# Evictions into column order, walked rows outside before and columns outside after

## The chip, the cores and the metric

The kernel runs on one core of a Trainium2 chip. The metric is the device time in microseconds (us). Three runs of the kernel before gave 1960.73, 1961.32 and 1965.41 us; their median is 1961.32 us.

## The reference

One encoder layer on 1024 tokens of width 1024, in fp32. One input projection gives queries, keys and values for two attention branches and two gates. Branch A is a 2-D neighbourhood attention: the 1024 tokens are a grid of 16 rows and 64 columns, and each query sees a window of 8 rows by 16 columns. Branch B is a windowed attention over token order. The gated sum goes through an output projection and a layer norm, and then a mixture of 16 experts with a second layer norm.

```
proj = einsum('bsd,de->bse', x, w_in) + b_in
qa, ka, va, qb, kb, vb, ga, gb = split(proj)
ya = neighbourhood_attention(qa, ka, va, rpb)      # tokens as 16 rows x 64 columns
yb = windowed_gqa(qb, kb, vb, sink)
mix = sigmoid(ga) * (ya @ w_branch_a) + sigmoid(gb) * (yb @ w_branch_b)
h   = layer_norm(alpha * x + mix @ w_out)
out = layer_norm(alpha * h + expert_choice_moe(h))
```

## The kernel before, in words

Every large product is made in three passes of float32r matmuls: an operand is split into a high part, rounded to float32r, and a low part, the rest; high x high, high x low and low x high are added in one PSUM bank. So each operand has to be written twice: ScalarE (ACT) writes the high part, and VectorE (DVE) then subtracts it from the source and writes the low part.

The first part of the kernel, up to about 575 us, makes the projections and both attentions at once. A unit of projection (`proj`, L183) is 24 matmuls of 512 columns into one PSUM tile `pj` of a pool of two (`pp`), so the next unit but one cannot start before the evictions of a unit have been read. `fill(n)` puts n projection matmuls between two steps of the attentions; the order on TensorE (PE) is that of the program, while ACT and DVE are ordered by the framework's scheduler. Branch B's steps come first, those of branch A after them, and the projections for branch A's four head pairs (i = 0 to 3) run beside the attention steps before they are needed.

Branch A wants its tokens in column order: position 16 * column + row, so that 128 neighbouring positions are 8 whole columns of the grid. The projection gives row order. The reordering is done by the evictions: `pj` for half `nh` holds rows 8 * nh to 8 * nh + 7, each of 64 columns, so that one column's eight rows lie 64 floats apart in PSUM and next to each other in the SBUF tile. The evictions concerned are

- `kside` (L208 ACT writing `khh`, L210 DVE writing `kll`): for each key unit and each of its halves of 64 partitions two ACT and two DVE instructions of 512 elements; a tile with keys of branch B (`kB`) uses the same lines without a reordering;
- `qside` (L217 ACT, L218 DVE, writing `qs`): for each query unit four of each with 256 elements; the queries of branch B have 512 elements in plain order;
- `va_unit` (L281 ACT, writing `vta`): one instruction of 512 elements in all 128 partitions for each value unit.

After the attentions, `y_load` (L595 ACT writing `yh`, L596 DVE writing `yl`) brings branch A's result back to row order while it is split, from SBUF to SBUF, in four tiles of 128 x 1024. Branch B's four tiles go through the same lines in plain order.

Of the kernel before, what the change touches and what calls it, by code (L numbers as in the profile page):

```python
# [21 lines left out]
HD = 64  # L22
GRID = 64
# [31 lines left out]
def encoder_block(ctx, tc, x, w_in, b_in, rpb, sink, w_branch_a, w_branch_b, w_out, ln1_g, ln1_b,  # L55
# [21 lines left out]
    def f32(ap):  # L77
        return ap.bitcast(F32)
# [98 lines left out]
    def proj(c, nh):  # L177
        hi, lo = held["w", c]
        ps = pp.tile([P, 512], F32, name="pj")
        n = 0  # L180
        for a, part in ((hi, "hi"), (hi, "lo"), (lo, "hi")):
            for k in range(KD):
                nc.tensor.matmul(ps, a[:, k, :], xT[part, nh][:, k, :], start=(n == 0), stop=(n == 3 * KD - 1))  # L183
                n += 1
                yield ps
# [10 lines left out]


    def by_column(ap, nh):
        return ap.rearrange("p (c r) -> p r c", r=16)[:, 8 * nh:8 * nh + 8, :]

    def by_row(ap):
        return ap.rearrange("p (r c) -> p r c", c=GRID)

    def kside(ps, c, half, khh, kll, view, src_view):
        lo, hi = half * HD, (half + 1) * HD
# [7 lines left out]
    def qside(src, c, half, qs, view):  # L213
        lo, hi = half * HD, (half + 1) * HD
        o = 1 - half
        b = bcol[lo:hi, c:c + 1]
        nc.scalar.activation(view(qs[lo:hi]), src, AF.Identity, bias=b)  # L217
        nc.vector.scalar_tensor_tensor(view(qs[o * HD:(o + 1) * HD]), src, b, f32(view(qs[lo:hi])),  # L218
                                       op0=ALU.add, op1=ALU.subtract)

    def k_unit(key, c, nh):
        if nh == 0:
            held[key] = ([qkv.tile([P, S], F32R, name="khh", tag="k", bufs=6) for _ in range(2)],
                         [qkv.tile([P, S], F32R, name="kll", tag="k", bufs=6) for _ in range(2)])
        for ps in proj(c, nh):
            yield
        for half in range(2):
            if key == "kB":
                v, sv = lambda ap: ap[:, nh * 512:(nh + 1) * 512], lambda ap: ap
            else:  # L230
                v, sv = lambda ap: by_column(ap, nh), by_row
            kside(ps, c, half, held[key][0][half], held[key][1][half], v, sv)
        done.add((key, nh))
# [11 lines left out]
    def qa_unit(key, c, nh):  # L245
        if nh == 0:
            held[key] = {(half, g): qkv.tile([P, 512], F32R, name="qs", tag="q", bufs=8)
                         for half in range(2) for g in range(2)}
        for ps in proj(c, nh):
            yield  # L250
        for half in range(2):
            for g in range(2):
                src = by_row(ps[half * HD:(half + 1) * HD])[:, :, 32 * g:32 * g + 32]
                qside(src, c, half, held[key][half, g], lambda ap: by_column(ap, nh))
        done.add((key, nh))

# [18 lines left out]
    def va_unit(key, c, nh):  # L275
        if nh == 0:
            held["vt", key] = vtp.tile([P, S], F32, name="vta")
        vt = held["vt", key]
        for ps in proj(c, nh):
            yield  # L280
        nc.scalar.activation(by_column(vt, nh), by_row(ps), AF.Identity, bias=bcol[:, c:c + 1])  # L281
        if nh:
            later.append([8, lambda: v_split(key, vt, 0, [(key, 0)])])
            later.append([14, lambda: v_split(key, vt, 4, [(key, 1)])])
# [37 lines left out]
    def qkv_units(i):  # L322
        return units(qa_unit, ("q", i), i) + units(k_unit, ("k", i), 4 + i) + units(va_unit, ("v", i), 8 + i)
# [184 lines left out]
    for r in range(16):  # L508
# [3 lines left out]
                                    ap=[[15 * 31, 8], [1, 8 * 31]]))  # L512
# [75 lines left out]
    def y_load(nm, src):  # L588
        for k in range(4):
            raw = gp.tile([P, S], F32, name="yraw", tag="g")  # L590
            nc.sync.dma_start(raw, src[k * P:(k + 1) * P, :])
            s0, hi, lo = raw, yT[nm][0][k], yT[nm][1][k]
            if nm == "a":
                s0, hi, lo = raw.rearrange("p (c r) -> p r c", r=16), by_row(hi), by_row(lo)
            nc.scalar.activation(hi, s0, AF.Copy)  # L595
            nc.vector.tensor_tensor(lo, s0, f32(hi), op=ALU.subtract)  # L596

    y_load("b", yb_d)
    wbr = {}

# [43 lines left out]

    gate("b", 0)
    y_load("a", ya_d)
    for d in range(0, 8, 2):
        work = [(nm, d + u) for u in range(2) for nm in ("b", "a")]
# [586 lines left out]
    def stats(t):  # L1235
        z, stt = total(t), stat.tile([P, 16], F32, name="ln")
        for h in range(2):
            nc.vector.bn_stats(stt[:, 6 * h:6 * h + 6], z[h])  # L1238
        yield
        nc.vector.bn_aggr(stt[:, 12:14], stt[:, :12].rearrange("p (c k) -> p c k", k=6))  # L1240
        yield
        nc.vector.tensor_scalar(stt[:, 14:15], stt[:, 13:14], EPS, None, op0=ALU.add)
        nc.gpsimd.tensor_tensor(stt[:, 15:16], stt[:, 14:15], mhalf, op=ALU.pow)
        yield
        for h, sl in enumerate(halves):
            nc.vector.scalar_tensor_tensor(accs[t][:, sl], z[h], stt[:, 12:13], g2[:, sl], op0=ALU.subtract,  # L1246
                                           op1=ALU.mult)
            if h == 0:
                yield
        yield  # L1250
        if t in TX:
            nc.scalar.activation(accs[t], accs[t], AF.Copy, scale=stt[:, 15:16])
            (nc.gpsimd if t in TP else nc.vector).tensor_tensor(accs[t], accs[t], b2, op=ALU.add)
        for sl in halves if t not in TX else [slice(0, D)]:
            if t not in TX:
                nc.vector.scalar_tensor_tensor(accs[t][:, sl], accs[t][:, sl], stt[:, 15:16], b2[:, sl], op0=ALU.mult,  # L1256
                                               op1=ALU.add)
            (nc.scalar if t % 2 else nc.sync).dma_start(out2[t * P:(t + 1) * P, sl], accs[t][:, sl])
        yield

    with tc.manual_schedule(engines=MAN):
        g = [stats(t) for t in range(8)]
# [30 lines left out]
```

## Time and profile before

| | |
|---|---|
| median of three runs | 1961.32 us |
| profiled execution | 1960.38 us, its span 1958.6 us |
| PE busy | 1863.8 us, 95% of the span |
| DVE, ACT, POOL busy | 1482.2, 1222.5, 221.3 us |
| projections and attentions | about 0 to 575 us |
| branches, mixing, first layer norm, routing | about 575 to 820 us |
| experts and the end | about 820 to 1958 us |

The table is read from the top: PE is busy nearly all the time, so what counts is where it waits or runs slowly. Those places are found in the stretches of the span and in the list of its waits.

### The profile page before, as it was taken

The page shows a single profiled execution, that of the slowest core. Times are in us where ns is not written, and L with a number is a line of the kernel's source. Part 1 is how long each engine was busy: PE and PEld are TensorE (multiplying, and loading weights), DVE is VectorE, ACT ScalarE, POOL GpSimd, SP SyncE. Part 2 cuts the span into 40 slices and gives each one's busy share as a digit, 9 for nine tenths or more (in the row PEclk, how much of TensorE's full clock was granted, in tenths as well). Part 3 has the DMA queues.
Part 4 walks back from the last instruction along what each step waited for, and adds up shares of the span by engine and source line. Part 5 has one row for each costly group of instructions (what it writes and reads, how often), then busy time and mean ns, then how long its engine had stood idle before and what let it go on. Part 6 is the DMA issues. An engine that isn't in the chain of part 4 may idle for free.

```text
span 1958.6 us, 23860 instructions
## 1 busy us (share of the span) xinstructions
PE 1863.8 (95%) x8795; PEld 1532.0 (78%) x8795; DVE 1482.2 (76%) x1857; ACT 1222.5 (62%) x1319; POOL 221.3 (11%) x271
## 2 busy tenths in 40 slices
PE   7998998988999999499999999999999999999996
PEld 6886877876877787388888888888888888888884
DVE  5466655554444558889989998998899899899897
ACT  4456655565444411277777777777777777777772
POOL 2121121111102222000000000000000000000003
PEclk9999999999999999699999999999999999999998
DMA  7111122222155274679999999999999999999982
GB/s 247 49 60 43 54 73 59 71 68 60 60 167 199 97 272 158 255 282 363 387 389 389 371 393 393 375 384 389 387 373 387 394 382 384 384 383 382 389 318 86
DMA packets 177129, 507.08 MB, mean 259 GB/s; under 512 B 12690, under 2 KB 55956, under 8 KB 177012
## 3 DMA queue, kind: packets, MB, share of 16 engines
q1 hardware_dynamic: 158816, 465.60, 63.5%
q0 software_dynamic: 7888, 24.13, 4.4%
q10 hardware_dynamic: 10308, 15.82, 2.4%
q8 instruction: 69, 1.13, 0.2%
q14 instruction: 48, 0.39, 0.1%
HBM read 468.40 MB, written 37.09 MB: 258 GB/s over the span
## 4 chain that ended last, share of the span: by engine, by line
PE 56%; DVE 2%; DMA 1%; issue 0%; ACT 0%; DVEq 0%; ACTq 0%
PE gu L1090 35%; PE yb L1090 18%; PE mt L1070 2%; PE gu L1098 1%; DMA xg<-h_d,idx 0%; DVE ln L1238 0%; DVE raw L1246 0%; DVE raw L1256 0%; DMA acc_d<-xr 0%; PE gu L1229 0%; PE mt L982 0%; DVE srt L752 0%; DVE srt L740 0%; DVE srt L750 0%; DVE srt L741 0%
## 5 line engine op out<-in xcount | busy, mean ns | idle before, releaser
L1053 DVE TENSOR_TENSOR mlo<-raw,mhi 128x2048 fp32r<-128x2048 f32 x383 | 859.1, 2277 | 52.8 <-PE yb L1090 26.0
L1045 ACT ACTIVATE mhi<-raw 128x2048 fp32r<-128x2048 f32 x383 | 732.3, 1912 | 200.3 <-PE gu L1090 93.7
L1090 PE MATMUL gu<-mhi,xsh 128*128 128x512 f32 x1008 | 398.2, 395 | 0.0
L1090 PE MATMUL gu<-mhi,xsl 128*128 128x512 f32 x1008 | 393.0, 390 | 0.0
L1090 PE MATMUL gu<-mlo,xsh 128*128 128x512 f32 x1008 | 393.0, 390 | 0.0
L1090 PEld LDWEIGHTS gu<-mhi,xsl 128*128 128x128 f32 x1008 | 189.5, 188 | 39.8 <-DVE xsl L1073 0.2
L1090 PEld LDWEIGHTS gu<-mlo,xsh 128*128 128x128 f32 x1008 | 189.7, 188 | 37.3
L1090 PEld LDWEIGHTS gu<-mhi,xsh 128*128 128x128 f32 x1008 | 189.6, 188 | 37.5 <-ACT xsh L1072 0.2
L1090 PE MATMUL yb<-mhi,hsl 128*128 128x512 f32 x512 | 199.4, 389 | 0.0
L1090 PE MATMUL yb<-mhi,hsh 128*128 128x512 f32 x512 | 199.3, 389 | 0.0
L1090 PE MATMUL yb<-mlo,hsh 128*128 128x512 f32 x512 | 199.2, 389 | 0.0
L183 PE MATMUL pj<-xThi,whi 128*128 128x512 f32 x544 | 157.1, 414 | 20.6 <-DVE kll L210 16.2
L183 PE MATMUL pj<-xTlo,whi 128*128 128x512 f32 x544 | 153.3, 405 | 0.0
L183 PE MATMUL pj<-xThi,wlo 128*128 128x512 f32 x544 | 151.3, 402 | 0.0
L183 PEld LDWEIGHTS pj<-xThi,whi 128*128 128x128 f32 x544 | 101.2, 195 | 43.9 <-issue 15.6
L183 PEld LDWEIGHTS pj<-xThi,wlo 128*128 128x128 f32 x544 | 99.3, 189 | 19.1
L183 PEld LDWEIGHTS pj<-xTlo,whi 128*128 128x128 f32 x544 | 98.6, 189 | 18.3
L1090 PEld LDWEIGHTS yb<-mhi,hsl 128*128 128x128 f32 x512 | 96.1, 188 | 20.0
L1090 PEld LDWEIGHTS yb<-mlo,hsh 128*128 128x128 f32 x512 | 96.1, 188 | 20.0
L1090 PEld LDWEIGHTS yb<-mhi,hsh 128*128 128x128 f32 x512 | 96.1, 188 | 19.9
L996 POOL DMA_INDIRECT xg<-h_d,idx x16 | 15.9, 993 | 810.1 <-DVE gsl L993 755.9
L1124 POOL DMA_INDIRECT acc_d<-yt,idx x15 | 39.3, 2618 | 211.3 <-ACT yt L1123 211.3
(264 smaller groups left out, 2392.6 us busy)
## 6 DMA issues: line engine op xcount, KB each, us to landing
raw<-in_w_up_dram SPq DMA_DIRECT2D x127, 1024.0 KB, 9.7
raw<-in_w_gate_dram SPq DMA_DIRECT2D x126, 1024.0 KB, 8.8
raw<-in_w_down_dram SPq DMA_DIRECT2D x126, 1024.0 KB, 9.1
wraw<-in_w_in_dram SPq DMA_DIRECT2D x34, 512.0 KB, 4.3
g_d<-gt SPq DMA_DIRECT2D x32, 256.0 KB, 2.3
sg<-g_d SPq DMA_DIRECT2D x16, 512.0 KB, 3.7
xt<-in_x_dram SPq DMA_DIRECT2D x8, 512.0 KB, 8.5
wraw<-in_w_out_dram SPq DMA_DIRECT2D x8, 512.0 KB, 5.3
```

The costliest lines, as they stand in the source:

```text
L183: nc.tensor.matmul(ps, a[:, k, :], xT[part, nh][:, k, :], start=(n == 0), stop=(n == 3 * KD - 1))
L996: nc.gpsimd.indirect_dma_start(out=xg, out_offset=None, in_=h_d, in_offset=bass.IndirectOffsetOnAxis(ap=idx[:, :1], axis=0))
L1045: nc.scalar.activation(hi[:, sl], src, AF.Copy)
L1053: nc.vector.tensor_tensor(lo[:, sl], src, f32(hi[:, sl]), op=ALU.subtract)
L1070: nc.tensor.transpose(pt[:, j, :], src[:, (4 * h + j) * P:(4 * h + j + 1) * P], ident)
L1090: nc.tensor.matmul(banks[b], a[:, k, :], ww[:, sl], start=(first and j == 0 and n == 0), stop=(last and j == len(w) - 1 and n == 2))
L1098: nc.tensor.matmul(bank, a[:, k, :], ww[:, sl], start=(k == 0 and n == 0), stop=(k == 7 and n == 2))
L1124: nc.gpsimd.indirect_dma_start(out=acc_d, out_offset=bass.IndirectOffsetOnAxis(ap=idx[:, :1], axis=0), in_=yt, in_offset=None, compute_op= ...
```

## The change

The views of both sides of an eviction swap their two inner dimensions. Before, an instruction goes through the rows of the grid outside and the 64 (or 32) columns inside: it reads PSUM in order and writes SBUF at every 16th float. After, it goes through the columns outside and the eight rows inside: it reads PSUM at every 64th float and writes SBUF in runs of eight floats, the next run 16 floats on. The same holds for the operand `khh` or `qs` that DVE subtracts, which lies in SBUF in the order of the output. In `y_load`, which uses the same helper, before the raw tile is read at every 16th float and `yh` is written in order; after, the raw tile is read in order and `yh` and `yl` are written at every 64th float, and DVE reads `yh` so too.

```
     def by_column(ap, nh):
-        return ap.rearrange("p (c r) -> p r c", r=16)[:, 8 * nh:8 * nh + 8, :]
+        return ap.rearrange("p (c r) -> p c r", r=16)[:, :, 8 * nh:8 * nh + 8]

     def by_row(ap):
-        return ap.rearrange("p (r c) -> p r c", c=GRID)
+        return ap.rearrange("p (r c) -> p c r", c=GRID)
...
-                src = by_row(ps[half * HD:(half + 1) * HD])[:, :, 32 * g:32 * g + 32]
+                src = by_row(ps[half * HD:(half + 1) * HD])[:, 32 * g:32 * g + 32, :]
...
             if nm == "a":
-                s0, hi, lo = raw.rearrange("p (c r) -> p r c", r=16), by_row(hi), by_row(lo)
+                s0, hi, lo = raw.rearrange("p (c r) -> p c r", r=16), by_row(hi), by_row(lo)
```

No instruction is added, removed or moved: on every engine the sequence is the same, and only the shapes of these instructions differ (64 x 8 x 64 becomes 64 x 64 x 8, and so on).

## Rows read from the trace of the kernel before

**Rows 1.** Stretches by stage: length, busy of PE, PEld, DVE, ACT, POOL, clock, DMA.
```profile
150.00:575.00 425.00, 392.37 (x1906) 322.42 (x1905) 223.43 (x509) 233.66 (x484) 70.17 (x124) 0.97 0.23 66
...
820.00:1950.00 1130.00, 1116.80 (x5183) 920.51 (x5180) 1009.70 (x687) 832.28 (x583) 70.21 (x43) 0.99 0.96 365
```
**Rows 2.** Same view, the stretches of 25 us between 150 and 575 with lowest clock.
```profile
175.00:200.00 25.00, 20.38 (x90) 15.85 (x89) 14.16 (x37) 14.36 (x33) 5.52 (x8) 0.86 0.10 30
...
325.00:350.00 25.00, 20.46 (x96) 16.85 (x95) 11.87 (x25) 11.86 (x23) 2.17 (x4) 0.93 0.15 48
...
400.00:425.00 25.00, 21.84 (x98) 18.55 (x99) 14.08 (x25) 12.28 (x23) 2.17 (x4) 0.86 0.22 63
...
475.00:500.00 25.00, 18.17 (x78) 14.45 (x77) 13.80 (x22) 13.19 (x20) 0.69 (x2) 0.86 0.11 31
```
**Rows 3.** PE's waits, 150 to 575 us: total us, times, longest.
```profile
PE pj L183 <- DVE kll L210: 15.9, 6, 4.5
PE pt L376 <- POOL sB L365: 5.8, 6, 3.8
PE sc L426 <- ACT khh L208: 2.9, 1, 2.9
PE pj L183 <- DVE qs L218: 2.5, 3, 1.4
PE sc L426 <- DVE kll L210: 1.6, 1, 1.6
PE pt L455 <- DVE pTA L459: 1.4, 1, 1.4
PE pt L260 <- ACT vta L281: 1.3, 1, 1.3
```
**Rows 4.** Evictions by line: plain (x8), reordered (x32), then by form; ns.
```profile
L208 ACT ACTIVATE khh<-pj,bcol x8: 682/684/687, 24.8 to 35.6; 64x512 fp32r<-64x512 f32 x8
L208 ACT ACTIVATE khh<-pj,bcol x32: 1107/1142/1177, 159.4 to 491.5; 64x512 fp32r<-64x512 f32 x32
L210 DVE SCALAR_TENSOR_TENSOR kll<-pj,bcol,khh x8: 733/750/757, 27.2 to 37.1; 64x512 fp32r<-64x512 f32 x8
L210 DVE SCALAR_TENSOR_TENSOR kll<-pj,bcol,khh x32: 1066/1106/1174, 163.6 to 493.8; 64x512 fp32r<-64x512 f32 x32
...
L217 ACT ACTIVATE qs<-pj,bcol 64x256 fp32r<-64x256 f32 x32 | 22.6, 706 | 19.8 <-DVE qs L218 14.7 <-PE pj L183 4.4
L218 DVE SCALAR_TENSOR_TENSOR qs<-pj,bcol,qs 64x256 fp32r<-64x256 f32 x32 | 21.2, 662 | 10.7 <-ACT qs L217 10.0
L281 ACT ACTIVATE vta<-pj,bcol 128x512 f32<-128x512 f32 x8 | 9.2, 1156 | 1.6 <-PE pj L183 1.4
```
**Rows 5.** Timeline, key units of head pairs 1 to 3: start, us, engine, instruction, [idle before].
```profile
308.96 2.27 ACT L208 ACTIVATE khh<-pj,bcol 64x512 fp32r<-64x512 f32 x2 [2.73 <-PE pj L183]
...
318.26 1.86 PE L183 MATMUL pj<-xThi,whi 128*128 128x512 f32 x7 [2.26 <-DVE kll L210]
...
321.08 2.32 ACT L208 ACTIVATE khh<-pj,bcol 64x512 fp32r<-64x512 f32 x2
...
330.37 2.04 PE L183 MATMUL pj<-xThi,whi 128*128 128x512 f32 x4 [4.54 <-DVE kll L210]
...
403.16 2.50 PE L183 MATMUL pj<-xThi,whi 128*128 128x512 f32 x5 [3.57 <-DVE kll L210]
...
484.81 0.47 PE L183 MATMUL pj<-xThi,whi 128*128 128x512 f32 x1 [2.30 <-DVE kll L210]
```
**Rows 6.** Run lengths in SBUF: the sorting line, runs of 64 down to 1; ns.
```profile
L741 DVE TENSOR_TENSOR srt<-srt x53: 186/207/216, 743.8 to 813.5; 16x64 f32<-16x64 f32 x28, 48x64 f32<-48x64 f32 x13, 80x64 f32<-80x64 f32 x12
```
**Rows 7.** The way back: a plain and a reordered `yh`, then PE's waits for it.
```profile
581.39 1.05 ACT L595 ACTIVATE yh<-yraw 128x1024 fp32r<-128x1024 f32 x1
...
584.72 1.97 ACT L595 ACTIVATE yh<-yraw 128x1024 fp32r<-128x1024 f32 x1
...
PE z L624 <- ACT yh L595: 5.0, 4, 1.3
```

## The prediction

> **What bounds the kernel now.** I read the stretches by stage first, then the stretches of 25 us, then the list of PE's waits, then the evictions by line, and last the timeline around the longest waits. The stages show where the evictions can matter. From 820 us on PE is busy for 1116.8 of 1130 us [rows 1], and nothing that the change touches is there; that stage should only begin earlier or later. From 150 to 575 us, where all the reordered evictions of keys, queries and values lie, PE is busy for 392.4 of 425 us [rows 1]: some 33 us are lost there in waiting. [...]
>
> The list of waits names the losses [rows 3]. PE waits 15.9 us in six places until DVE has written `kll`, since only then is a `pj` tile free for the next projection; 2.9 and 1.6 us for the last `khh` and `kll` ahead of the scores; 2.5 us for `qs`, 1.3 for `vta`, 1.4 for a `pTA` that stands behind a `kll` on DVE. The longest wait for POOL's normalization, 3.8 us, lies at the end of head pair 0's key units, whose `kll` stand on DVE ahead of the maxima that this softmax needs. That is 29.4 us (15.9 + 2.9 + 1.6 + 2.5 + 1.3 + 1.4 + 3.8) in which PE waits for reordered evictions or for what is queued behind them.
>
> Why an eviction is late is seen in two rows of the same line: `khh` takes 684 ns where it is written in plain order and 1142 ns where it is written at every 16th float; `kll` takes 750 and 1106 ns [rows 4]. ACT and DVE take turns on one `pj` tile (two `khh`, 2.27 us together, then two `kll`, and so again for the other half) [rows 5]. So a reordered key unit is four of each one after another: 4 x 1.142 + 4 x 1.106 = 8.99 us.
>
> **The change part by part.** No instruction is added, removed or moved, and no wait is added. What changes is the time of 32 `khh`, 32 `kll`, 32 `qs` on either engine, 8 `vta`, and 4 `yh` and 4 `yl`.
>
> *The SBUF side.* The extra time per element is (1142 - 684)/512 = 0.89 ns on ACT and (1106 - 750)/512 = 0.70 ns on DVE [rows 4]. The rows of `yh`, which touches no PSUM, give (1970 - 1050)/1024 = 0.90 ns [rows 7], the same as ACT's above. So what costs now is the step of 16 floats in SBUF, on the reading side as on the writing side. After the change SBUF gets runs of eight floats. The sorting line works on runs of 64 down to single elements two floats apart, always 64 elements, and all its 53 instructions take 186 to 216 ns [rows 6]; a cost of 0.7 ns per element would add 45 ns. I take runs of eight as free.
>
> *The PSUM side.* No row shows a PSUM read at steps, so I bound it. Below: it is free, and the evictions take plain time, 684 and 750 ns. Below that there is nothing to gain, since plain order is the best that either line shows. Above: it costs what the step costs in SBUF, so that all stays at 1142 and 1106 ns; or more, since another memory need not be as good. How much headroom is there? From 820 us on PE writes 512 fp32 per partition into PSUM in 1116.8/5183 = 0.215 us at most [rows 1], 0.42 ns each, while the plain slope of the evictions (a plain instruction of 684 ns less a fixed part of 270 ns, which the two reordered forms of 706 ns for 256 and 1142 for 512 elements give) is (684 - 270)/512 = 0.81 ns. PSUM is thus shown to move twice what ACT asks of it, and a step that cost two elements' worth of that pace (0.84 ns) would not be felt; one that cost four (1.68 ns) would leave the time as it is. I take the lower end, 684 and 750 ns: it is the nearest row by line and shape, and of the two memories only SBUF has shown a penalty.
>
> [...]
>
> *Sum of the evictions.* A key unit gets shorter by 4 x 0.458 + 4 x 0.356 = 3.26 us. Queries: (0.89 + 0.70) x 256 = 0.41 us for each pair of instructions, 1.63 us a unit. Values: 1.156 - 0.684 = 0.47 us a unit. ACT and DVE have slack in this stage (233.7 and 223.4 of 425 us busy) [rows 1], so only what PE waits for counts.
>
> *What of PE's waits goes.* By head pair. Pair 0 has 15.9 - 2.26 - 4.54 - 3.57 - 2.30 = 3.2 us of waits for `kll` and the 3.8 us for POOL behind them [rows 3, 5]; its two units shorten by 6.5 us, of which I take 6.0. Pair 1 waits 2.26 us behind its first unit and 4.54 behind the second [rows 5]: 6.5 of 6.8 us go. Pair 2 waits 1.4 (`pTA`) and 3.57 us, both within its first unit: 3.3 of 5.0 go. Pair 3 waits 2.30, 2.9 and 1.6 us behind its first unit and the first half of its second: 3.26 + 1.63 = 4.9 of 6.8 go. Together 20.7 us. The waits for `qs` are at most 1.4 us each, less than a query unit's 1.63, so all 2.5 us go. Of the wait for `vta` 0.5 us goes. Sum: 23.7 us.
>
> *The clock.* The four stretches lose 25 x (0.14 + 0.07 + 0.14 + 0.14) = 12.3 us at full speed [rows 2], and each holds one of the longest waits (3.8, 4.54 and 3.57 us, and pair 3's three in 6 us). With these gone or under 2 us the clock should hold in three of the four: 12.3 - 3.5 (one stretch at 0.86) = 8.8 us.
>
> *What is late next.* PE will come sooner to the steps whose softmax is on ACT, DVE and POOL. The waits for POOL other than the longest are 5.8 - 3.8 = 2.0 us now [rows 3]; I charge 3 us for their growth.
>
> *The way back.* `yh` and `yl` change a read at every 16th float for a write at every 64th. Both are steps in SBUF, and I leave them at 1.97 us. If the longer step were free, the four would give back up to 4 x 0.92 = 3.7 us of the 5.0 us that PE waits for them [rows 7]; if it cost twice as much, those 3.7 us would be added. Both ends go into the range.
>
> Sum: 23.7 + 8.8 - 3 = 29.5 us. The profiled execution took 1960.4 us, 0.9 us under the median of the runs, so both serve alike: 1960.4 - 29.5 = 1931 us.
>
> **The rivals.** *The penalty only changes sides*: steps in PSUM cost like steps in SBUF, about 1.7 ns per element. [...] Against it: PSUM's pace above. Time 1958 to 1963, say 1960.
>
> *One engine alone gains*: DVE, which reads two streams and writes a third in the new order, stays at 1106 ns, ACT goes to 684. A key unit then shortens by 1.83 us and not 3.26, so 56% of the 23.7 us, 13 us, and I give it half of the clock, 4 us, less the 3 us: 1946 us. Nothing in the rows asks for it, but nothing shows these three streams together.
>
> *PSUM steps are dearer than SBUF steps* (the slower side). It decides from about 1.7 ns per element, where the evictions begin to be longer than now. At 2.5 ns each `khh` and `kll` gains 0.8 x 512 = 0.41 us, a key unit 3.3 us; PE already waits behind seven of the eight units, so nothing hides it: 7 x 3.3 = 23 us, some 3 us for queries, and 4 us or more in clock: about 1990 us. For it: steps of 256 bytes are longer than any in the rows. Against it: PSUM's pace again.
>
> That the change does not do what it says is excluded by the instructions' shapes, which are 64 x 64 x 8 now.
>
> **How the numbers follow.** The likeliest case has 0.57, one engine alone 0.10, the penalty that changes sides 0.20, dearer steps 0.13. The likeliest has its own range: from 1960 - 29.4 - 12.3 = 1919 us, where all waits and all clock come back, to 1945, where some 15 us do. The range of 1919 to 1964 adds the one-engine case and the unchanged one, and leaves dearer steps out. A measurement of this kernel can tell 0.3% from no change, about 6 us: faster by more than that are the first two cases, 0.67; within it the third, 0.20; slower the last, 0.13.
>
> **What would show it.** `khh` near 0.68 us and `kll` near 0.75, `qs` near 0.48 on both engines, and `vta` near 0.69 say that PSUM steps are free; 1.14 and 1.11 that the penalty moved. If the evictions are short, PE's waits for `kll` should be a few us in all, and the stretches at 175, 325 and 400 us should have a clock near 1.00. The stage of the experts should keep its length. The forecast is wrong if the evictions are short and the waits stay, which would mean that another chain, the softmax over POOL above all, ends just behind them.

## The result and the profile after

The changed kernel took 1930.39 us (median of 4 runs, 1929.42 to 1934.31) against 1962.65 us for the kernel before: a ratio of 0.9838 with a 95% interval of 0.9819 to 0.9858. Its profiled execution has a span of 1927.8 us, 30.8 us less than the 1958.6 us before.

The stages come first. The lines show length, busy time of PE, PEld, DVE, ACT and POOL, then clock, DMA share and GB/s, with the stretches set where the same work now lies.

```profile
150.00:551.00 401.00, 388.29 (x1924) 320.96 (x1922) 210.98 (x514) 213.78 (x488) 70.17 (x130) 0.99 0.25 75
...
790.00:1920.00 1130.00, 1116.04 (x5176) 920.03 (x5176) 1010.54 (x686) 832.05 (x583) 70.51 (x43) 0.99 0.96 365
```

Against [rows 1], the stage of the experts is as long and as busy as before and merely begins earlier: its first expert matmul starts at 798.7 us, before at 829.5, and from there to the end of the span it is 1129.1 us in both. The attention stage lost most of its idle time: PE is busy for 388.3 of 401 us there, before for 392.4 of 425, so 12.7 us of idle time are left of 32.6.

The evictions of the changed kernel, by line, with minimum, median and maximum in ns over the plain and the reordered ones together:

```profile
L208 ACT ACTIVATE khh<-pj,bcol x40: 667/684/692, 24.5 to 461.6; 64x512 fp32r<-64x512 f32 x40
...
L210 DVE SCALAR_TENSOR_TENSOR kll<-pj,bcol,khh x40: 733/750/759, 26.9 to 463.6; 64x512 fp32r<-64x512 f32 x40
...
L217 ACT ACTIVATE qs<-pj,bcol x48: 458/472/685, 50.0 to 417.8; 64x256 fp32r<-64x256 f32 x32, 64x512 fp32r<-64x512 f32 x16
...
L218 DVE SCALAR_TENSOR_TENSOR qs<-pj,bcol,qs x48: 476/490/756, 50.7 to 418.3; 64x256 fp32r<-64x256 f32 x32, 64x512 fp32r<-64x512 f32 x16
...
L281 ACT ACTIVATE vta<-pj,bcol x8: 662/690/693, 178.3 to 429.4; 128x512 f32<-128x512 f32 x8
```

Set beside [rows 4], the 32 reordered `khh` and `kll` can no longer be told from the 8 plain ones: all 40 lie within 667 to 692 and 733 to 759 ns. PE's waits in the changed kernel up to the end of the attentions (total us, times, longest):

```profile
PE pj L183 <- DVE kll L210: 3.5, 2, 2.9
PE pt L376 <- POOL sB L365: 3.0, 4, 2.4
PE sc L426 <- ACT khh L208: 1.3, 1, 1.3
PE sc L426 <- DVE kll L210: 1.2, 1, 1.2
PE pt L260 <- ACT vta L281: 0.9, 1, 0.9
PE sc L346 <- DVE mx L348: 0.4, 1, 0.4
PE po L466 <- DVE yA L473: 0.3, 1, 0.3
```

They sum to 10.6 us; the same list before, [rows 3] with 0.9 us of smaller entries, to 32.3. The waits for `qs` are gone, those for `kll` at L183 fell from 15.9 to 3.5 us. And the stretches of 25 us, to be set beside [rows 2]:

```profile
175.00:200.00 25.00, 22.39 (x101) 17.95 (x100) 12.99 (x40) 12.90 (x32) 5.50 (x8) 0.86 0.11 32
325.00:350.00 25.00, 25.00 (x130) 21.05 (x128) 12.51 (x30) 12.94 (x28) 5.11 (x9) 1.00 0.23 65
375.00:400.00 25.00, 22.07 (x111) 17.99 (x110) 14.99 (x31) 15.04 (x32) 4.32 (x8) 1.00 0.19 60
450.00:475.00 25.00, 22.54 (x110) 18.23 (x109) 13.56 (x28) 13.70 (x28) 3.20 (x7) 1.00 0.15 43
```

Only the first of the four is still below full clock. Before, all stretches between 150 and 575 us lost 14.0 us of full-speed time (12.3 in [rows 2], and 1.8 at clocks of 0.96 and 0.97 from 225 to 275 us); after, 25 x 0.14 = 3.5 us. Waits and clock together: 32.3 - 10.6 + 14.0 - 3.5 = 32.2 us, close to the 30.8 us by which the span fell. The sum is a little too large, because some of the low clock falls into the waits and is counted twice: before, PE waits from 184 to 185.4 us while the granted clock is at 0.50.

### The profile page after: what moved, and what is told of

It is laid out like the page before. It is cut to its first block, busy times and chain, and to the rows that moved or that the text cites. A ratio compares the mean times of both kernels' runs of the same rounds, so it can differ in the third digit from the quotient of the medians.

```text
span 1927.8 us, 23860 instructions
## 1 busy us (share of the span) xinstructions
PE 1856.4 (96%) x8795; PEld 1528.4 (79%) x8795; DVE 1466.1 (76%) x1857; ACT 1197.8 (62%) x1319; POOL 220.7 (11%) x271
## 4 chain that ended last, share of the span: by engine, by line
PE 62%; DVE 4%; DMA 1%; ACT 0%; POOL 0%; issue 0%; DVEq 0%; ACTq 0%; POOLq 0%
PE gu L1090 36%; PE yb L1090 18%; PE po L807 4%; PE mt L1070 2%; DMA sg<-g_d 1%; PE gu L1098 1%; PE pl L850 0%; DMA xg<-h_d,idx 0%; DVE ln L1238 0%; POOL sg L628 0%; DVE raw L1246 0%; DVE raw L1256 0%; PE pt L842 0%; DVE srt L752 0%; DVE aff L856 0%
## 5 line engine op out<-in xcount | busy, mean ns | idle before, releaser
L183 PE MATMUL pj<-xThi,whi 128*128 128x512 f32 x544 | 153.1, 406 | 5.6 <-DVE kll L210 3.8
L183 PE MATMUL pj<-xTlo,whi 128*128 128x512 f32 x544 | 153.0, 405 | 0.0
L183 PE MATMUL pj<-xThi,wlo 128*128 128x512 f32 x544 | 150.8, 402 | 0.0
L183 PEld LDWEIGHTS pj<-xThi,whi 128*128 128x128 f32 x544 | 98.8, 190 | 26.1 <-DVE kll L210 3.4
L183 PEld LDWEIGHTS pj<-xThi,wlo 128*128 128x128 f32 x544 | 98.8, 188 | 18.9
L183 PEld LDWEIGHTS pj<-xTlo,whi 128*128 128x128 f32 x544 | 98.9, 190 | 18.4
```

## The experiments

Two theories were set against each other. *Chain*: ACT and DVE take turns on one `pj` tile, and PE waits for the end of that chain and for what stands behind it on the two queues. *Load*: ACT and DVE simply have less to do. "Before" below is the kernel before, run on the same chip.

**Only the keys new.**

```
-                v, sv = lambda ap: by_column(ap, nh), by_row
+                v, sv = lambda ap: new_column(ap, nh), new_row
```

> Only the key evictions walk columns outside; queries, values and the way back are as in the kernel before. Theory (chain: PE waits for the last eviction of a key unit, because the pj tiles come free one after another, and for little else): the key units shorten by 3.26 us each, nearly the whole gain stays, the waits for qs (2.5 us) and 0.4 us for vta come back: 1931 to 1937 us. Rival (load: what counts is the ACT and DVE time saved, 26 of 43 us being the keys'): 61% of the gain of 32 us, 1943 us.

Measured: 1938.5 us, ratio 0.9879 (0.9863 to 0.9896), 23.6 us less than before. That is just outside the chain's range and 4.5 us below the load's time, so between the two, nearer to the chain's. The waits for `kll` are 3.5 us, as in the changed kernel; back are 2.4 us for `qs`, 1.4 for `vta` and 4.6 for POOL.

**Only the keys old**, the complement.

```
-                v, sv = lambda ap: by_column(ap, nh), by_row
+                v, sv = lambda ap: old_column(ap, nh), old_row
```

> The complement: queries, values and the way back are new, the key evictions are as before. Chain theory: only the waits for qs and part of the one for vta go, 3 us, and no long wait, so the clock stays where it was: 1955 to 1960 us. Load rival: 39% of 32 us, 1950 us or less.

Measured: 1955.03 us, ratio 0.9961 (0.9947 to 0.9975), 7.1 us less than before: at the lower edge of the chain's range, and 5 us above the load's. The two parts nearly add up to the gain of the result: 23.6 + 7.1 = 30.7 of 32.3 us. Three quarters of it are the keys'.

**Of the keys, only ACT's part.**

```
-            nc.scalar.activation(view(khh[o * HD:(o + 1) * HD]), src, AF.Identity, bias=b)
+            nc.scalar.activation(nview(khh[o * HD:(o + 1) * HD]), nsrc, AF.Identity, bias=b)
```

> Of the kernel before, only the 32 khh of the keys on ACT walk columns outside; kll on DVE stays at 1.11 us. Chain theory: the two engines take turns, so a key unit shortens by ACT's part alone, 1.83 of 3.26 us: 56% of the waits tied to the keys (some 10 of 17.5 us) and perhaps half of the clock's 10 us: 1943 to 1949 us. Rival (the slower engine sets the pace): DVE still takes 1.11 us for each, no gain, 1960 us. Rival (load): 14.7 of 43 us, 1951 us.

Measured: 1951.38 us, ratio 0.9947 (0.9930 to 0.9964), 10.7 us less: a smaller gain than the chain's 1943 to 1949 us, and what the load theory said. `khh` took 682 ns and the reordered `kll` 1113. So one engine alone gains, which refutes the pace of the slower one, but this run does not tell chain from load. In the trace the waits of head pairs 1 and 3 shrank as a chain shorter by 1.83 us asks (2.26 and 4.54 us became 0.46 and 2.70; the three of pair 3 became 0.46, 2.06 and 1.80). The wait for POOL behind pair 0 stayed at 3.81 us, and of pair 2's 5.0 us 4.2 remained.

**What a step costs on either side**, with the gates' evictions in 16 patterns.

```
+            src, dst = ps.rearrange("p (a b) -> p b a", b=n), gt.rearrange("p (b a) -> p b a", b=n)   # step n in PSUM
...
+            dst, src = gt.rearrange("p (a b) -> p b a", b=n), ps.rearrange("p (b a) -> p b a", b=n)   # step n in SBUF
...
+            dst = gt.rearrange("p (a b k) -> p b a k", b=16 // k, k=k)                                # runs of k, 16 apart
```

> The changed kernel with its 32 gate evictions (128x512, PSUM to SBUF) in 16 patterns, each once on ACT and once on DVE; the gates come out permuted within a tile, so the output is another and only the durations are read. Plain: 0.69 us on ACT, about 0.70 on DVE. Theory (a PSUM read costs nothing at any step): steps of 2, 4, 8, 16, 32, 64 and 256 floats in PSUM all at the plain time. Rival (PSUM pays at some steps, and 64 with runs of eight was lucky): 1.1 us at one or more of them. On the SBUF side: steps of 2 free, steps of 4 or more floats near 1.14 us, and among the runs 16 floats apart those of 8 and 4 free, runs of 2 between.

ACT's instructions in order of time (start, us, engine, line, instruction): plain; a step of 2 in SBUF; 2 in PSUM; 4 in SBUF; 8 in SBUF; then runs of two; 64 in PSUM; runs of four; 256 in PSUM; runs of eight.

```profile
74.22 0.69 ACT L303 ACTIVATE gt<-pj,bcol 128x512 f32<-128x512 f32 x1
88.72 0.73 ACT L303 ACTIVATE gt<-pj,bcol 128x512 f32<-128x512 f32 x1 [4.06 <-PE pj L183]
107.83 0.67 ACT L303 ACTIVATE gt<-pj,bcol 128x512 f32<-128x512 f32 x1
...
201.99 1.17 ACT L303 ACTIVATE gt<-pj,bcol 128x512 f32<-128x512 f32 x1
...
283.55 1.32 ACT L303 ACTIVATE gt<-pj,bcol 128x512 f32<-128x512 f32 x1 [0.96 <-PE pj L183]
...
487.15 0.71 ACT L303 ACTIVATE gt<-pj,bcol 128x512 f32<-128x512 f32 x1 [2.06 <-PE pj L183]
...
501.33 0.69 ACT L303 ACTIVATE gt<-pj,bcol 128x512 f32<-128x512 f32 x1 [3.26 <-PE pj L183]
516.31 0.69 ACT L303 ACTIVATE gt<-pj,bcol 128x512 f32<-128x512 f32 x1 [1.32 <-PE pj L183]
529.56 0.69 ACT L303 ACTIVATE gt<-pj,bcol 128x512 f32<-128x512 f32 x1 [0.94 <-PE pj L183]
546.64 0.69 ACT L303 ACTIVATE gt<-pj,bcol 128x512 f32<-128x512 f32 x1 [1.50 <-PE pj L183]
```

Steps of 4, 8, 16, 32 in PSUM took 0.69, 0.69, 0.69 and 0.67 us, steps of 16 and 64 in SBUF 1.16 and 1.18. On DVE it was alike: every PSUM step 0.74 to 0.75 us, as plain; SBUF steps of 4, 8, 16 and 64 took 1.14, 1.24, 1.09 and 1.15. So a read of PSUM is free at any step tried, on both engines. On the SBUF side, where these patterns only write, it is enough that the floats are written in pairs that lie one or two floats apart: runs of two (0.71 us) and a step of 2 (0.73 us) are nearly as good as runs of eight. Each pattern stands for one instruction on each engine.

**The way back undone.**

```
-                s0, hi, lo = raw.rearrange("p (c r) -> p c r", r=16), by_row(hi), by_row(lo)
+                s0, hi, lo = raw.rearrange("p (c r) -> p r c", r=16), old(hi), old(lo)
```

> The changed kernel with the way back (yh and yl) as before: reads at every 16th float, writes in order. Theory (both are steps in SBUF and cost alike): yl goes from 2.18 back to 2.00 us, yh stays at 1.97, PE's waits for yh stay near 5 us, the same time as the changed kernel within 0.1%. Rival (the new direction helped by freeing DVE or ACT): 3 to 4 us slower.

For this run, the next one and the last one of this section, which share a chip, the changed kernel ran there once more.

> The changed kernel once more, on the same chip as the next three, so that these can be set against it: 1929 to 1934 us.

Measured: the changed kernel 1934.65 us, ratio 0.9858 (0.9840 to 0.9875), which is just above what was expected and 26.0 us less than the kernel before on that chip, where the result had 32.3; with the way back undone 1932.25 us, ratio 0.9846 (0.9829 to 0.9863). The intervals overlap, no difference can be told, and nothing shows that the new direction helped. On DVE the new direction is dearer, as the first reordered `yl` of either kernel shows, first the kernel before:

```profile
587.12 2.00 DVE L596 TENSOR_TENSOR yl<-yraw,yh 128x1024 fp32r<-128x1024 f32 x1
```

and the changed kernel:

```profile
553.39 2.00 ACT L595 ACTIVATE yh<-yraw 128x1024 fp32r<-128x1024 f32 x1
555.65 2.18 DVE L596 TENSOR_TENSOR yl<-yraw,yh 128x1024 fp32r<-128x1024 f32 x1
```

PE never waits for `yl`, only for `yh` (5.4 and 5.3 us in the two).

**A third `pj` tile in the kernel before**, taken from the transposes, which keep two of three.

```
-    pp = att.enter_context(tc.tile_pool(name="pp", bufs=2, space=PSUM))
+    pp = att.enter_context(tc.tile_pool(name="pp", bufs=3, space=PSUM))
-    ptp = att.enter_context(tc.tile_pool(name="ptp", bufs=3, space=PSUM))
+    ptp = att.enter_context(tc.tile_pool(name="ptp", bufs=2, space=PSUM))
```

> The kernel before with three pj tiles and two in place of three for the transposes; evictions as slow as before. If PE waits because a pj tile is not free, a third tile takes most of the 15.9 us for kll at L183 and the 2.5 us for qs away without any faster eviction, against new waits at the transposes: 1940 to 1955 us. If the evictions' own load counts, no gain or a loss from the transposes: 1960 to 1970 us.

Measured: 1963.82 us, ratio 1.0009 (0.9996 to 1.0022): nothing gained. Its list of PE's waits:

```profile
PE pt L455 <- DVE pTA L459: 9.6, 6, 3.1
PE pt L376 <- POOL sB L365: 6.6, 6, 4.6
PE sc L426 <- ACT khh L208: 5.4, 1, 5.4
PE sc L346 <- DVE mx L348: 3.5, 1, 3.5
PE sc L426 <- DVE mx L431: 2.6, 2, 1.4
```

All waits for `pj` are gone, 18.4 us with those for `qs`, and nearly as much has turned up at the transposes (`pTA`), the scores (`khh`, `mx`) and POOL: DVE's `pTA` and maxima stand in order behind the `kll` of a chain that is still 9 us long. Head pair 3 shows it without the transposes: its three waits, 2.30 us for a `pj` tile, 2.9 and 1.6 us ahead of the scores [rows 3, 5], became two ahead of the scores, 5.41 and 1.62 us. For the other pairs the cause is not shown, since the wait for `pTA`, 1.4 us before and 9.6 us here, is one for a transpose tile, and this run has one of those less; a third `pj` tile without that loss was not tried.

**The chain shortened in another way**, in both kernels: the second copies of `khh` and `kll` are made from the first ones in SBUF, after both halves' reads of PSUM.

```
-        for o in (half, 1 - half):
-            nc.scalar.activation(view(khh[o * HD:(o + 1) * HD]), src, AF.Identity, bias=b)
-        for o in range(2):
-            nc.vector.scalar_tensor_tensor(view(kll[o * HD:(o + 1) * HD]), src, b, f32(view(khh[lo:hi])), ...)
+        nc.scalar.activation(view(khh[lo:hi]), src, AF.Identity, bias=b)
+        nc.vector.scalar_tensor_tensor(view(kll[lo:hi]), src, b, f32(view(khh[lo:hi])), ...)
...
+        nc.scalar.activation(view(khh[lo2:hi2]), f32(view(khh[lo:hi])), AF.Copy)
+        nc.vector.tensor_copy(view(kll[lo2:hi2]), f32(view(kll[lo:hi])))
```

In the kernel before:

> The kernel before, still walking rows outside, with the second copies of khh and kll taken from the first ones in SBUF, after both halves' reads of PSUM. If the moment at which a pj tile is released is what counts (release theory), two of each stand before it, some 4.5 us in place of 9: the 15.9 us of waits for kll at L183 go nearly all, about 1940 us. If the time that the evictions take on the in-order queues of ACT and DVE counts (queue theory), whatever comes behind them is as late as before, since the copies step through SBUF too and are no shorter: the waits turn up at the scores and transposes, 1955 to 1963 us. A mixture: in between, by the share of waits at L183 that do not turn up elsewhere.

Measured: 1934.53 us, ratio 0.9865 (0.9849 to 0.9882), 27.8 us less than before, with every reordered eviction still stepping through SBUF. Of its 15.9 us of waits for `kll` at L183 little is left (total us, times, longest):

```profile
PE pj L183 <- DVE kll L208: 1.6, 2, 1.1
```

Its first key unit of head pair 1 on the timeline (start, us, engine, line, instruction):

```profile
303.58 1.14 ACT L207 ACTIVATE khh<-pj,bcol 64x512 fp32r<-64x512 f32 x1 [2.73 <-PE pj L183]
304.75 1.13 ACT L214 ACTIVATE khh<-khh 64x512 fp32r<-64x512 f32 x1
304.75 1.13 DVE L208 SCALAR_TENSOR_TENSOR kll<-pj,bcol,khh 64x512 fp32r<-64x512 f32 x1 [0.96 <-ACT khh L207]
305.92 0.61 DVE L215 CAST kll<-kll 64x512 fp32r<-64x512 f32 x1
306.32 1.14 ACT L207 ACTIVATE khh<-pj,bcol 64x512 fp32r<-64x512 f32 x1
307.49 1.17 ACT L214 ACTIVATE khh<-khh 64x512 fp32r<-64x512 f32 x1
307.49 1.19 DVE L208 SCALAR_TENSOR_TENSOR kll<-pj,bcol,khh 64x512 fp32r<-64x512 f32 x1 [0.51 <-ACT khh L207]
308.72 0.62 DVE L215 CAST kll<-kll 64x512 fp32r<-64x512 f32 x1
```

ACT copies in SBUF while DVE reads PSUM, so the engines take turns only for the first copies: the unit ends 5.8 us after its start where the taking of turns in [rows 5] made it 9. My two theories for this run, release and queue, were no real alternatives, since this edit shortens both: a tile is released after two instructions of either engine, and the chain is shorter too, DVE's copies taking 0.61 us where I had put them at no less than a `kll`. Which of the two counts is left open. But it decides the first question: ACT still needs 1.14 us for each of its 32 instructions and DVE saves only 7 us in its `kll` over the kernel, and yet nearly the whole gain is there. The load theory falls.

In the changed kernel:

> The changed kernel with the second copies of khh and kll taken from the first ones in SBUF, after both halves' reads of PSUM: only two ACT and two DVE instructions stand before the release of a pj tile in place of four of each. Chain theory: of the waits left (3.5 us for kll, 2.5 us for khh and kll ahead of the scores, 2.4 us for POOL behind head pair 0) the first go and the others hardly move: 1924 to 1929 us. Rival (what is left is the load of ACT and DVE, which hardly changes, or their order): 1930 to 1934 us.

Measured: 1922.71 us, ratio 0.9801 (0.9785 to 0.9818), which lies clear of the changed kernel's 0.9840 to 0.9875 on the same chip: 12 us better, a little beyond the chain theory's range, and the best version found. Not all of it is the chain's. The spans of the two profiled executions differ by 6.3 us (1932.9 and 1926.6), of which 5.1 us are PE's waits up to the end of the attentions, 11.3 us in the one and 6.2 in the other; the rest of the 12 us was not traced to waits. The granted clock differs too: its mean over an execution was 0.981 or 0.982 in the four runs of the changed kernel on this chip and 0.983 to 0.986 in the five of this one. The waits for `pj` are gone altogether, and what is left is spread:

```profile
PE pt L382 <- POOL sB L371: 3.1, 7, 1.7
PE sc L432 <- ACT khh L214: 1.2, 1, 1.2
PE pt L266 <- ACT vta L287: 0.9, 1, 0.9
PE sc L432 <- DVE kll L215: 0.7, 1, 0.7
```

## Why the prediction was right

The forecast was 1931 us with a range of 1919 to 1964; the time was 1930.4. The mechanism was as foreseen. That the number came within 1 us is luck: the terms below miss by 2 to 4 us each and largely cancel, and the same kernel took 1934.65 us in its second measurement.

*The SBUF side and the PSUM side.* Both as taken. `khh` 684 ns, `kll` 750, `vta` 690, and `qs` 472 and 490 with the plain ones of branch B in the medians: the lower bound in every line. The run with the 16 patterns shows it more widely: no step in PSUM cost anything, up to 256 floats (0.67 to 0.69 us on ACT, 0.74 to 0.75 on DVE), while the penalty of SBUF begins between a step of 2 floats and one of 4: steps of 2 and runs of 2 took 0.71 to 0.76 us on either engine, steps of 4 took 1.14 to 1.17. The headroom that I worked out for PSUM came from PE's writes, which are in order, and said nothing of reads at steps; that the lower bound would hold was a choice, and the runs bore it out.

*What of PE's waits goes.* The direction was right and the size too large: 20.3 us in place of 23.7. By head pair the waits of the changed kernel are these:

```profile
179.60 2.15 PE L376 MATMUL pt<-ident,sB 128*128 128x128 f32 x4 [2.35 <-POOL sB L365]
...
313.94 1.17 PE L183 MATMUL pj<-xThi,whi 128*128 128x512 f32 x4 [0.55 <-DVE kll L210]
...
382.58 1.43 PE L183 MATMUL pj<-xThi,whi 128*128 128x512 f32 x5 [2.93 <-DVE kll L210]
...
459.43 0.38 PE L426 MATMUL sc<-khh,qs 128*128 128x256 f32 x1 [1.31 <-ACT khh L208]
...
460.97 0.39 PE L426 MATMUL sc<-kll,qs 128*128 128x256 f32 x1 [1.16 <-DVE kll L210]
```

Pair 0 lost 4.7 of 7.0 us (6.0 forecast), pair 1 6.3 of 6.8 (6.5), pair 2 2.0 of 5.0 (3.3), pair 3 4.4 of 6.8 (4.9). The step that was mis-sized is the one that lets a whole unit's 3.26 us come off the wait behind it. Pair 2 shows what it left out, on DVE (start, us, engine, line, instruction):

```profile
379.74 1.23 DVE L104 TENSOR_TENSOR wlo<-wraw,whi 128x1024 fp32r<-128x1024 f32 x1 [0.23 <-issue]
...
381.00 1.53 DVE L210 SCALAR_TENSOR_TENSOR kll<-pj,bcol,khh 64x512 fp32r<-64x512 f32 x2
```

The weights' split (`wlo`, 1.23 us) stands in DVE's order ahead of the second pair of `kll`, as the split's other part (`whi`, 1.05 us) stands in ACT's ahead of the second pair of `khh`. So this unit took 7.3 us, from 375.23 to 382.53, where four `khh` and four `kll` alone are 5.7 us. The chain is made of the engine's whole queue, and other work in it does not get shorter.

*What is late next.* I charged 3 us for growing waits for POOL; they shrank, from 2.0 to 0.7 us. The change in the queries or values did that, not the one in the keys: these waits were 2.2 us with only the keys new and 0.7 with only the keys old. In the second profile of the changed kernel they were 1.3 us. This error and the last one cancel within 1 us.

*The clock.* Foreseen 8.8 us, measured 10.5: 8.8 in the four stretches and 1.8 in two that I had not counted. That three of four would hold was right in this execution, but not which: I had expected it at 175, 325 and 400 us, and the one that stayed at 0.86 was that at 175, behind the 2.35 us wait for POOL, while pair 3's held. The sum came out the same because both had lost 3.5 us before. Nor is three of four a law, as the last section shows.

*The way back.* As taken: `yh` took 2.00 us, and PE waited 4.9 us for it in place of 5.0.

*The rivals.* "One engine alone" did not happen. Made to happen for the keys it gave 1951 us; its 1946 had the queries and values in it too, so that run does not test the figure. "The penalty only changes sides" and "dearer steps" are refuted by the evictions of the changed kernel and by the patterns.

## What to carry to other kernels

When an fp32 eviction must reorder, let it step through PSUM and write SBUF in runs of at least two floats: here 128x512 took 0.67 to 0.75 us at any step tried in PSUM and 0.71 to 0.76 us in runs of two in SBUF, but 1.09 to 1.32 us at steps of 4 to 64 floats in SBUF. When two engines take turns on one PSUM tile, price the sum of their turns (9 us a key unit before), with what stands between them, and shorten it, by cheaper instructions (1938.5 us) or by taking second copies out of it (1934.53 us), before adding buffers: here a further tile, taken from another pool, moved the waits and gained nothing (1963.82 us). Why ACT and DVE take turns even where they read different partitions of the tile no run here shows; letting them read the two halves at once was not tried. Price a wait by everything that stands in the waiting engine's order, not only by the instructions that the change touches: pair 2's unit took 7.3 us where its own evictions are 5.7.

## What the runs showed of the hardware

A step of 8 floats in SBUF was dearer than any other, larger ones included: 1.32 us on ACT and 1.24 on DVE against 1.16 and 1.09 for a step of 16, with one instruction of each on either engine.

The same wait does not always cost the clock. In the second profile of the changed kernel the waits were the same within 0.1 us (2.35, 0.55, 2.93, 1.29 and 1.15), but the granted clock fell in more stretches:

```profile
175.00:200.00 25.00, 21.95 (x107) 17.93 (x106) 13.31 (x41) 13.56 (x35) 5.50 (x8) 0.93 0.11 32
375.00:400.00 25.00, 22.07 (x102) 18.16 (x101) 14.26 (x29) 14.11 (x29) 4.33 (x8) 0.93 0.15 46
450.00:475.00 25.00, 22.55 (x103) 18.29 (x102) 13.61 (x28) 12.45 (x27) 4.12 (x8) 0.93 0.19 50
```

Three stretches at 0.93 lose 5.3 us where the first profile's one at 0.86 lost 3.5. That is 1.8 of the 5.1 us between the spans, 1932.9 and 1927.8 us; over the whole kernel the mean granted clock was 0.981 against 0.985. The four runs of the result go the same way: 1929.42 and 1929.53 us at a mean clock of 0.985, 1931.26 at 0.983, 1934.31 at 0.981. Around the same wait of 2.93 us the mean granted clock from 375 to 400 us was 1.00 in one execution and 0.93 in the other, so some of the difference between two times of one kernel is the clock's: 1.8 us here.
